# A woven delta rule whose four compute engines follow one written order, with weights split in halves at fixed steps and residual tiles lent out as buffers

## The chip, the cores and the metric

The kernel runs on one core of a Trainium2 chip. The metric is the device time of one execution in microseconds. Five queues matter here: TensorE (PE; its weight loads are listed as PEld), VectorE (DVE), ScalarE (ACT), GpSimd (POOL), and SyncE (SP), which issues the transfers. Each takes its own instructions in the order in which they stand; they meet only through semaphores.

## The reference, cut to what matters

Three transformer blocks of width 1024 on 512 tokens, in float32. The change lies inside the second block, in the gated delta rule and in the products around it:

```
h = layer_norm(x, ln_in_g, ln_in_b)
pool_in, qkv, z, beta_raw, a_raw, gate_a, gate_b = split(h @ w_in)
y_a = multiscale_pool(pool_in) * pool_scale
qkv = silu(causal_depthwise_conv(qkv));  q, k = l2norm(q), l2norm(k)       # 8 heads of 128
u, w = triangular_solve(I + strict(k_beta k^T * decay), [v beta, k_beta e^gc])
for chunk in chunks:                                                       # the recurrence
    v_new = u - w S;  o = qg S + attn v_new;  S = S e^gl + kg^T v_new
y_b = rms_norm(o) * o_norm_w * silu(z)
mixed = sigmoid(gate_a) * y_a + sigmoid(gate_b) * y_b
h = layer_norm(alpha * h + mixed @ w_out, ln1_g, ln1_b)
```

## The kernel before, in words

Activations stand with the 1024 features in eight tiles of 128 partitions and the 512 tokens along the free axis; `X` holds the residual, `hx` the normalized input as pairs of a rounded part and its remainder. A product with a 1024 x 128 block of weights is a **job** of `K.gemm`: for each of eight feature tiles (k-steps) three matmuls of 512 columns (L172 to L174: rounded weights by both parts of the input, remainder of the weights by the rounded part), 24 in all. Its 512-KB block of weights comes through SP into `wst` (two buffers) and is split in two halves of 512 columns: ACT rounds a half into `wh` (L156), POOL takes the remainder into `wl` (L157). There are four buffers of each, that is two jobs' worth.

`block2` runs the delta rule as a weave. `Weave` is a planner that executes while the program is written: generators (`scores`, `tokens`, `blocks`, `inverse`, `recur`, one chain each over the eight heads, and `conv_silu`, `l2`, `out_norm`, `gate` for single tiles) yield the time at which their next step may stand, computed with costs such as `W.on("V", 0.85)`; `W.pe` moves the planner's clock. Steps that are due go first, by rank, and between them the jobs of `JOBS` go k-step by k-step as filler. `JOBS` names 46 jobs: `k`, `q`, `v` of each head, `z` and `g` (the two gates of a head's output), `a2` to `a7` (gate of the pooled part). A job may have a `need`: `k` and `q` of head h wait for the recurrence of head h-4, `v` for `tokens` of head h-1, `z` and `g` for the normalized output.

Before, `tc.manual_schedule` holds only PE and DVE to that order. ACT, POOL and SP are put in order by the scheduling layer, which has its own idea of when things are ready, and `K.wunit` asks for weights early with a raised priority.

Steps that the prediction uses, by line of the profile:

- `conv_silu`: ACT copies the job's PSUM into `cz` (L1379) and scales it into `QK` or `vT` (L1381), after which the PSUM bank is free; three DVE multiply-adds (L1384); Tanh (L1387). `cz` is a new tile each time, whose first three columns POOL clears (L1378).
- `l2`: Square and a rounding on ACT (L1404, L1407), remainder on POOL (`sl`, L1409), two matmuls of column sums (L1411, L1412); for the second of a head's pair a Ln over both (L1419) and two Exp (L1421), each kind behind a table load.
- `inverse`: transposes and products in PSUM `piv` (L1544 to L1573), with copies on ACT (`Xi` L1546, `Yi` L1569) and masks or subtractions on DVE.
- `recur`: per chunk of 128 tokens L1593, DVE, L1599, ACT `vn` (L1603), L1607, DVE `S`, L1616 and L1618 into `po`; its small products go to the one PSUM bank `prc`.
- `out_norm`: copy and Square on ACT (L1629, L1631), the sum over features into `prc` (L1634), Ln and Exp (L1636, L1637) behind a table load each, a multiply on DVE.
- `gate`: Tanh from PSUM into the one buffer `mt` (L1647); for `z` a DVE multiply that reads the PSUM (L1655), then POOL.

PSUM holds two banks `g` for the jobs, two `piv`, two for the sums `m`, one `prc`, one `po`.

Of the kernel before, what the change touches and what calls it, by code (L numbers as in the profile page):

```python
# [9 lines left out]
F32 = mybir.dt.float32  # L10
# [26 lines left out]
JOBS = "k0 q0 v0 k1 q1 a2 a3 v1 k2 q2 a4 v2 k3 q3 a5 v3 z0 k4 q4 g0 v4 z1 k5 q5 g1 v5 z2 k6 q6 g2 v6 k7 q7 z3 v7 g3 z4 g4 z5 g5 a6 z6 g6 a7 z7 g7"  # L37
# [1184 lines left out]
def block2(K, X, entry, es):  # L1222
# [11 lines left out]
    hx = []  # L1234
    for k in range(NT + 1):
        if k == EV[0]:
            for u, o in zip(units, head):
                entry.norm.evict(u, o[:u[0].shape[0]])
        if k < NT:
            affine(K, entry.norm, "ln_in_g", "ln_in_b", hx, k)  # L1240

# [128 lines left out]
    nc.vector.tensor_scalar(ow, K.v("o_norm_w"), 0.25, None, op0=MUL)  # L1370
    W = Weave()
    sums = []
    QK, vT, ci, oTs, mixed = {}, {}, {}, {}, {}

    def conv_silu(ps, ti, y):
        yield W.now + 0.25
        z = pH.tile([P, 3 + T], F32, tag="cz", name=K.nm("cz"))
        nc.gpsimd.memset(z[:, :3], 0.0)  # L1378
# [4 lines left out]
        for k in range(3):  # L1383
            nc.vector.scalar_tensor_tensor(y, v4(z[:, k:k + T]), w(k), y, op0=MUL, op1=ADD)  # L1384
            yield W.on("V", 0.85)
# [6 lines left out]
    def l2(h, y, bias):  # L1392

        if not sums:
            ps = K.pp.tile([P, 2, T], F32, tag="m", bufs=1, name=K.nm("pm"))
        else:
            ps = sums[0][0]
        n = len(sums)
        sums.append((ps, y, bias))
        both = list(sums)  # L1400
        if n:
            sums.clear()
# [7 lines left out]
        yield W.on("P", 1.35)  # L1410
        nc.tensor.matmul(ps[:, n], lhsT=ones_r, rhs=sh, start=True, stop=False)  # L1411
        nc.tensor.matmul(ps[:, n], lhsT=ones_r, rhs=sl, start=False, stop=True)  # L1412
        t = W.pe(0.46)
        W.mark(("sum", h, n), t)
        if not n:
            return
        yield ("sum", h, 0)
        yield t
        nc.scalar.activation(ps, ps, AF.Ln, scale=0.25, bias=K.eps[1e-6])  # L1419
        for k, (ps, y, bias) in enumerate(both):  # L1420
            nc.scalar.activation(ps[:, k], ps[:, k], AF.Exp, scale=-0.5, bias=bias)  # L1421
        yield W.on("A", 5.0)
        for k, (ps, y, bias) in enumerate(both):
            nc.vector.tensor_tensor(y, y, v4(ps[:, k]), MUL)
        W.mark(("QK", h), W.on("V", 1.4))

    def head_in(h, o, ps):

        if o == "v":
            vT[h] = ht("vT", VTB)  # L1430
# [3 lines left out]
        if h not in QK:  # L1434
            QK[h] = pH.tile([P, 4, 2, P], F32, tag="QK", bufs=4, name=K.nm("QK"))
# [8 lines left out]
    def scores(h):  # L1444
# [14 lines left out]
        qk = QK[h]  # L1459
        MT = MTs[h] = ht("MT")  # L1460
# [25 lines left out]
    def tokens(h):  # L1486

        if h > 1:
            yield ("r", h - 2)
        qg = ht("qg")  # L1490
        nc.sync.dma_start(qg, rd[1, h].partition_broadcast(P))
        yield ("QK", h)
        KG = ht("KG")
        VB = ht("VB")
# [21 lines left out]
    def blocks(h):  # L1516
# [6 lines left out]
        for a in range(SB - 1):  # L1523
# [3 lines left out]
            w = W.on("V", 0.42)  # L1527
# [4 lines left out]
    def inverse(h):  # L1532
# [7 lines left out]
        yield W.on("V", 1.2)  # L1540
# [39 lines left out]
    def recur(h):  # L1580
# [6 lines left out]
        O = K.ps("o")  # L1587
        S = None
        for c in range(4):
# [25 lines left out]
            if c:  # L1615
                nc.tensor.matmul(O[:, cc[c]], lhsT=S, rhs=qg[:, cc[c]], start=True, stop=False)  # L1616
                W.pe(0.23)
            nc.tensor.matmul(O[:, cc[c]], lhsT=vn, rhs=AT[:, cc[c]], start=c == 0, stop=True)  # L1618
# [6 lines left out]
    def out_norm(h, O):  # L1625
# [4 lines left out]
        s = K.tmp()  # L1630
        nc.scalar.activation(s, oT, AF.Square)  # L1631
        yield W.on("A", 1.3) + 0.4
        ps = K.ps("rc")
        nc.tensor.matmul(ps, lhsT=K.ones, rhs=s, start=True, stop=True)  # L1634
        yield W.pe(0.86)
        nc.scalar.activation(s, ps, AF.Ln, scale=1.0 / 128, bias=K.eps[1e-6])  # L1636
        nc.scalar.activation(s, s, AF.Exp, scale=-0.5)  # L1637
        yield W.on("A", 3.9)
# [4 lines left out]
    def gate(h, o, ps):  # L1643

        yield W.now + 0.25
        t = ht("mt", MTB)
# [27 lines left out]
    def products(jobs):  # L1674
# [3 lines left out]
        def fetch(j):  # L1678
            for e, us in (("A", 1.3), ("P", 2.8)):
                W.on(e, us)  # L1680
            return K.wunit(I[wname[j[0]]][int(j[1])])
        w = fetch(jobs[0])
        for n, (o, h) in enumerate(jobs):
            h = int(h)
            need = ("o", h) if o in "zg" else ("r", h - 4) if o in "kq" and h > 3 else ("A", h - 1) if o == "v" and h else 0.0
# [4 lines left out]
            nxt = fetch(jobs[n + 1]) if n + 1 < len(jobs) else None  # L1690
            ps = K.gps()
            for k in range(NT):
                K.gemm(ps, hx[k:k + 1], w, off=k * P, first=k == 0, last=k == NT - 1)
                W.pe(0.68)
                if k < NT - 1:
# [3 lines left out]
            w = nxt  # L1699

    with tc.manual_schedule(engines={mybir.EngineType.PE, nc.vector.engine}):
# [6 lines left out]
    mixed = [mixed[h] for h in range(NT)]  # L1708
    K.psum(g=5, m=3)
# [542 lines left out]
```

## Time and profile before

| | us |
|---|---|
| median of 3 runs (2886.43 to 2895.01) | 2893.02 |
| the profiled execution | 2890.26 |
| its span | 2888.5 |
| the weave: first matmul of `k0` to the first of `w_out` | 1111.2 to 1560.6 = 449.4 |

The profiled execution's span is 1.8 us below its own time. The page shows PE at 92% of the whole span and at 6 to 9 tenths in the slices of the weave; in the long products before and after it, PE is at 9 in every slice. PE's busy time is modelled and matmuls overlap, so what is read below is the time in which PE stands idle, what released it, and the granted clock.

### The profile page before, as it was taken

How to read it: one execution, taken by the hardware profiler on the slowest of the kernel's cores; microseconds unless marked ns; L12 is line 12 of the kernel's file. 1: busy time of each engine (PE TensorE's matmuls, PEld its weight loads, DVE VectorE, ACT ScalarE, POOL GpSimd, SP SyncE). 2: the span in 40 equal slices, each digit the busy share in tenths (PEclk: the TensorE clock that was granted, in tenths of full speed). 3: DMA queues.
4: the chain of work that ended last, by engine and by line, in shares of the span. 5: the costliest groups of instructions: out<-in, count | busy, mean ns of one | idle time of the engine just before them, and what ended most of it. 6: DMA issues, size and time to landing. Idle time of an engine off the chain costs nothing.

```text
span 2888.5 us, 34202 instructions
## 1 busy us (share of the span) xinstructions
PE 2667.2 (92%) x12206; PEld 2132.6 (74%) x12206; DVE 1734.2 (60%) x2731; ACT 1308.1 (45%) x2375; POOL 1364.5 (47%) x1071
## 2 busy tenths in 40 slices
PE   7899999599999988889789999999888889999997
PEld 5677777478888866767677788877666678788885
DVE  7889889975342495865853811125877765422246
ACT  4357776433222355556444533332556642322234
POOL 6554432454444454535535544454544344444442
PEclk9999999799999999999999999999999899999999
DMA  3321111132322222222222222232322122222222
GB/s 115 114 86 48 55 44 37 60 116 91 98 96 95 90 73 88 89 74 74 81 60 75 80 95 95 95 110 80 108 83 73 44 81 88 95 95 95 95 95 102
DMA packets 79193, 243.32 MB, mean 84 GB/s; under 512 B 11312, under 2 KB 15320, under 8 KB 79024
## 3 DMA queue, kind: packets, MB, share of 16 engines
q1 hardware_dynamic: 79024, 241.15, 25.6%
q8 instruction: 96, 1.57, 0.2%
q14 instruction: 73, 0.60, 0.1%
HBM read 230.96 MB, written 4.52 MB: 82 GB/s over the span
## 4 chain that ended last, share of the span: by engine, by line
PE 39%; DVE 10%; ACT 2%; issue 1%; POOL 1%; DMA 0%; DVEq 0%; SPq 0%; ACTq 0%; POOLq 0%
PE pg L173 12%; PE pg L172 12%; PE pg L174 12%; DVE p L2061 1%; DVE Z L1526 1%; DVE Zt L1525 0%; DVE X L396 0%; DVE A L2009 0%; PE piv L1551 0%; DVE p L2058 0%; DVE z L2064 0%; POOL wl L157 0%; DVE QK L1384 0%; DVE X L1795 0%; ACT wh L156 0%
## 5 line engine op out<-in xcount | busy, mean ns | idle before, releaser
L157 POOL TENSOR_TENSOR wl<-wst,wh 128x512 fp32r<-128x512 f32 (+1 forms) x808 | 1094.8, 1360 | 1309.6 <-ACT wh L156 1219.6
L156 ACT ACTIVATE wh<-wst 128x512 fp32r<-128x512 f32 (+1 forms) x808 | 501.8, 627 | 1075.1 <-PE pg L173 930.7
L172 PE MATMUL pg<-op,wh 128*128 128x512 f32 (+1 forms) x2008 | 815.9, 407 | 53.5 <-ACT wh L156 20.9
L173 PE MATMUL pg<-op,wh 128*128 128x512 f32 (+1 forms) x2008 | 801.7, 400 | 1.8 <-DVE op L192 1.6
L174 PE MATMUL pg<-op,wl 128*128 128x512 f32 (+1 forms) x2008 | 798.1, 398 | 3.8 <-POOL wl L157 3.8
L172 PEld LDWEIGHTS pg<-op,wh 128*128 128x128 f32 (+1 forms) x2008 | 385.6, 192 | 135.1 <-ACT wh L156 21.5
L174 PEld LDWEIGHTS pg<-op,wl 128*128 128x128 f32 (+1 forms) x2008 | 384.8, 192 | 85.7 <-POOL wl L157 6.1
L173 PEld LDWEIGHTS pg<-op,wh 128*128 128x128 f32 (+1 forms) x2008 | 386.2, 192 | 80.4 <-DVE op L192 4.5
L172 PE MATMUL pg<-hid,wh 128*128 128x512 f32 x688 | 273.1, 397 | 1.3 <-DVE hid L191 1.3
L173 PE MATMUL pg<-hid,wh 128*128 128x512 f32 x688 | 273.0, 397 | 1.2 <-DVE hid L192 1.2
L174 PE MATMUL pg<-hid,wl 128*128 128x512 f32 x688 | 273.2, 397 | 0.0
L733 DVE SCALAR_TENSOR_TENSOR py<-z,vec,py 128x512 f32<-128x512 f32 x240 | 180.2, 751 | 10.9 <-ACT py L731 6.2
L1180 DVE TENSOR_TENSOR X<-X,pg 128x512 f32<-128x512 f32 x56 | 38.5, 688 | 226.9 <-PE pg L174 226.9
L172 PEld LDWEIGHTS pg<-hid,wh 128*128 128x128 f32 x688 | 129.9, 189 | 33.4 <-DVE hid L191 1.8
L173 PEld LDWEIGHTS pg<-hid,wh 128*128 128x128 f32 x688 | 129.9, 189 | 33.2 <-DVE hid L192 1.5
L174 PEld LDWEIGHTS pg<-hid,wl 128*128 128x128 f32 x688 | 129.9, 189 | 31.6 <-issue 0.2
L191 DVE CAST hid<-t 128x512 fp32r<-128x512 f32 x86 | 52.8, 614 | 146.3 <-ACT t L1157 145.6
L1171 DVE SCALAR_TENSOR_TENSOR t<-pg,R 128x512 f32<-128x512 f32 x32 | 22.1, 692 | 84.0 <-PE pg L174 83.9
L998 ACT ACTIVATE P<-ps,s 128x128 f32<-128x128 f32 (+3 forms) x128 | 66.3, 523 | 11.7 <-DVE s L997 9.7
L192 DVE TENSOR_TENSOR hid<-t,hid 128x512 fp32r<-128x512 f32 x86 | 64.6, 751 | 3.0
L997 DVE TENSOR_REDUCE s<-ps 128x1 f32<-128x128 f32 (+3 forms) x128 | 60.2, 483 | 8.2 <-PE ps L996 6.8
L1384 DVE SCALAR_TENSOR_TENSOR QK<-cz,vec,QK 128x512 f32<-128x512 f32 x48 | 50.0, 1053 | 17.5 <-DMA qg<-rowsd 11.3
(521 smaller groups left out, 4395.3 us busy)
## 6 DMA issues: line engine op xcount, KB each, us to landing
wst<-in_w_f_dram SPq DMA_DIRECT2D x64, 512.0 KB
wst<-in_w_up_dram SPq DMA_DIRECT2D x32, 512.0 KB
wst<-in_w_down_dram SPq DMA_DIRECT2D x32, 512.0 KB
wst<-in_w_ga_dram SPq DMA_DIRECT2D x24, 512.0 KB
wst<-in_w_fg_dram SPq DMA_DIRECT2D x22, 512.0 KB
wst<-in_w_fu_dram SPq DMA_DIRECT2D x22, 512.0 KB
wst<-in_w_q_dram SPq DMA_DIRECT2D x16, 512.0 KB
wst<-in_w_out_dram SPq DMA_DIRECT2D x16, 512.0 KB
```

Of the source, the lines that this page charges most:

```text
L156: nc.scalar.activation(h, st, AF.Copy)
L157: nc.gpsimd.tensor_tensor(l, st, h, SUB)
L172: self.nc.tensor.matmul(ps, lhsT=wh, rhs=h[:, sl], start=first and k == 0, stop=False)
L173: self.nc.tensor.matmul(ps, lhsT=wh, rhs=l[:, sl], start=False, stop=False)
L174: self.nc.tensor.matmul(ps, lhsT=wl, rhs=h[:, sl], start=False, stop=last and k == n - 1)
L191: nc.vector.tensor_copy(h, src)
L192: nc.vector.tensor_tensor(l, src, h, SUB)
L733: nc.vector.scalar_tensor_tensor(y, z[:, k:k + T], w(k), y, op0=MUL, op1=ADD)
L997: nc.vector.tensor_reduce(mx[:, h:h + 1], S[:, :L], AX, MAX, negate=True)
L998: nc.scalar.activation(Pt[h][:, :L], S[:, :L], AF.Exp, bias=mx[:, h:h + 1], accum_out=den[:, h:h + 1])
L1180: nc.vector.tensor_tensor(X[:, m], X[:, m], ps, ADD)
L1384: nc.vector.scalar_tensor_tensor(y, v4(z[:, k:k + T]), w(k), y, op0=MUL, op1=ADD)
```

## The change: what it does, and the diff

- ACT and POOL join PE and DVE in `manual_schedule`: all four keep the order in which the weave writes them. SP stays with the scheduling layer.
- A job's weights are no longer fetched by `K.wunit`. `load(n + 2)` issues the transfer at the start of job n; `split(n + 1, 0)` stands after k-step 0 of job n and `split(n + 1, 1)` after k-step 3.
- The layer-normed residual `X` is stored to DRAM (`xkept`) right after it is made and read back after the weave. Between, its eight tiles serve as two more `QK` buffers (six instead of four), a third `KG`, `VB` and `qg`, and a second `vT`. So `k` and `q` need the recurrence of head h-6 and `v` needs `tokens` of h-2.
- `cz` becomes two lasting tiles, cleared once: 2 clearings on POOL instead of 24.
- `out_norm` writes its sum to the bank of `po` and has its own tile `os`; `recur` takes `po` later, once the head before is through (`("n", h - 1)`). `gate` uses the ring of six `t` instead of `mt`.
- `l2` takes turns (`("turn", i)`), and `JOBS` runs `k4` to `v5` ahead of `z0`; the planner's DVE costs go from 0.85 to 1.0 (conv), 0.42 to 0.64 (a pair of `blocks`), 1.2 to 1.7 (`Yi`).

The instructions themselves are the same in number on PE (11963), DVE and ACT; POOL has 22 clearings less, SP 16 transfers of 256 KB more. From the norm behind the weave on, all queues stand as before.

```diff
-JOBS = "k0 q0 v0 k1 q1 a2 a3 v1 k2 q2 a4 v2 k3 q3 a5 v3 z0 k4 q4 g0 v4 z1 k5 q5 g1 v5 z2 k6 q6 g2 v6 k7 q7 z3 v7 g3 z4 ...
+JOBS = "k0 q0 a2 v0 k1 q1 a3 v1 k2 q2 a4 v2 k3 q3 a5 v3 k4 q4 v4 k5 q5 v5 z0 g0 k6 q6 z1 v6 g1 k7 q7 z2 v7 g2 z3 g3 z4 ...
...
             affine(K, entry.norm, "ln_in_g", "ln_in_b", hx, k)
+            nc.sync.dma_start(xkept[k], X[:, k])
...
+    xq = lambda k: X[:, k:k + 2].rearrange("p a t -> p (a t)").rearrange("p (c e t) -> p c e t", c=4, e=2)
+    QKs = [pH.tile([P, 4, 2, P], F32, bufs=1, name=f"QK{i}") for i in range(4)] + [xq(0), xq(2)]
+    three = lambda tag, k: [ht(f"{tag}{i}", 1) for i in range(2)] + [X[:, k]]
+    KGs, VBs, qgs = three("KG", 4), three("VB", 5), three("qg", 6)
+    vTs = [X[:, 7], ht("vT", 1)]
...
-        z = pH.tile([P, 3 + T], F32, tag="cz", name=K.nm("cz"))
-        nc.gpsimd.memset(z[:, :3], 0.0)
+        z = czs[0]
+        czs.reverse()
...
-            w = W.on("V", 0.42)
+            w = W.on("V", 0.64)
...
-        ps = K.ps("rc")
+        ps = K.ps("o")
         nc.tensor.matmul(ps, lhsT=K.ones, rhs=s, start=True, stop=True)
...
-        t = ht("mt", MTB)
+        t = K.tmp()
...
+        def split(n, k):
+            if n < len(jobs):
+                ws.setdefault(n, []).append(K.wsplit(st[n][:, k * WP:(k + 1) * WP]))
+                W.on("P", 1.35, W.on("A", 0.65))
...
-            need = ("o", h) if o in "zg" else ("r", h - 4) if o in "kq" and h > 3 else ("A", h - 1) if o == "v" and h else 0.0
+            need = ("o", h) if o in "zg" else ("r", h - 6) if o in "kq" and h > 5 else ("A", h - 2) if o == "v" and h > 1 else 0.0
...
-            nxt = fetch(jobs[n + 1]) if n + 1 < len(jobs) else None
+            load(n + 2)
+            w = ws.pop(n)
             ps = K.gps()
             for k in range(NT):
                 K.gemm(ps, hx[k:k + 1], w, off=k * P, first=k == 0, last=k == NT - 1)
                 W.pe(0.68)
+                if k in (0, 3):
+                    split(n + 1, k // 3)
...
-    with tc.manual_schedule(engines={mybir.EngineType.PE, nc.vector.engine}):
+    with tc.manual_schedule(engines={mybir.EngineType.PE, nc.vector.engine, nc.scalar.engine, nc.gpsimd.engine}):
...
+    for k in range(NT):
+        nc.sync.dma_start(X[:, k], xkept[k])
```

The orders of two places follow; line numbers of the changed kernel run 13 to 22 higher for the same step (L1381 is L1394, L1419 is L1433, L1599 is L1616, L1634 is L1655). The first is ACT around the first Ln and Exp of `l2` (on `pm`), before; `pg` is the PSUM of a job, `wh` a rounded half of weights:

```order
L1387 ACTIVATE t_2135_10027<-QK_2116_9942 128x512
L156 ACTIVATE wh_2131_10002<-wst_2128_9996 128x512
L1379 ACTIVATE cz_2134_10013<-pg_2122_9953 128x512
L1419 ACT_TABLE_LOAD
L1419 ACTIVATE pm_2103_9887<-pm_2103_9887,eps_1_79 128x1024
L156 ACTIVATE wh_2137_10043<-wst_2136_10041 128x512
L1421 ACT_TABLE_LOAD
L1421 ACTIVATE pm_2103_9887<-pm_2103_9887,lnk_9485 128x512
L1381 ACTIVATE QK_2116_9942<-pg_2122_9953,vec_87 128x4x128
L1421 ACTIVATE pm_2103_9887<-pm_2103_9887,lnq_9483 128x512
```

The same place in the changed kernel:

```order
L1394 ACTIVATE X_91<-pg_2111_9914,vec_87 128x512
L156 ACTIVATE wh_2126_9985<-wst_2110_9912 128x512
L156 ACTIVATE wh_2130_10011<-wst_2122_9963 128x512
L1433 ACT_TABLE_LOAD
L1433 ACTIVATE pm_2118_9955<-pm_2118_9955,eps_1_79 128x1024
L1435 ACT_TABLE_LOAD
L1435 ACTIVATE pm_2118_9955<-pm_2118_9955,lnk_9496 128x512
L1435 ACTIVATE pm_2118_9955<-pm_2118_9955,lnq_9494 128x512
L1392 ACTIVATE cz1_9752<-pg_2123_9965 128x512
L1394 ACTIVATE QK1_9755<-pg_2123_9965,vec_87 128x4x128
L1400 ACTIVATE t_2132_10027<-X_91 128x512
L156 ACTIVATE wh_2133_10032<-wst_2122_9963 128x512
```

Before, the two copies out of one PSUM bank (`cz`, `QK`) stood on both sides of the Ln and the first Exp, with a half of weights between; now the block stands whole, and both copies and the next half of weights stand behind it.

The second place is PE at the end of a stretch with no job to fill it, ahead of the first `v` job after it, before (`piv`, `prc`, `po`, `pm` are the PSUM banks named above):

```order
L1616 MATMUL po_2265_10642<-qg_2086_9771,S_2314_10814 128x128
L1618 MATMUL po_2265_10642<-AT_2144_10073,vn_2323_10840 128x128
L1411 MATMUL pm_2302_10781<-sh_2317_10826,onesr_9735 128x512
L1412 MATMUL pm_2302_10781<-sl_2318_10827,onesr_9735 128x512
L1497 MATMUL piv_2334_10872<-ident_73,QK_2180_10234 128x128 x4
L1573 MATMUL piv_2337_10890<-Yi_2326_10851,T1_2328_10860 128x128 x4
L1634 MATMUL prc_2339_10898<-t_2330_10866,ones_77 128x512
L1508 MATMUL piv_2340_10906<-ident_73,vT_2231_10478 128x128 x4
L1599 MATMUL prc_2342_10915<-VB_2201_10320,Yf_2338_10896 128x128
```

And the longest such stretch of the changed kernel, which stands between `g3` and `z4`; this is its second half:

```order
L1577 MATMUL piv_2714_12627<-T1_2711_12614,Yi_2707_12601 128x128 x4
L1515 MATMUL piv_2717_12638<-ident_73,QK1_9755 128x128 x4
L1585 MATMUL piv_2721_12650<-ident_73,Xi_2718_12644 128x128 x4
L1569 MATMUL piv_2723_12657<-Xi_2718_12644,MT_2569_12040 128x128 x4
L1655 MATMUL po_2724_12662<-os_2716_12634,ones_77 128x512
L1526 MATMUL piv_2728_12675<-ident_73,vT_2079_9764 128x128 x4
L1591 MATMUL piv_2729_12684<-Yi_2722_12655,T1_2725_12664 128x128 x4
L1616 MATMUL prc_2731_12697<-X_91,Yf_2730_12689 128x128
L1483 MATMUL piv_2735_12704<-QK1_9755 128x256 x2
L1624 MATMUL prc_2736_12707<-vn_2732_12699,X_91 128x128
```

The sum of `out_norm` (L1634, now L1655) has left `prc` for `po`, so the next head's first `prc` product (L1599, now L1616) no longer shares a bank with it. Before there are two such unfilled stretches, of 29 and 23 rows of chain products; now there are shorter ones, ahead of `v5`, `z3`, `z4`, `z5` and in `a6`, and the one ahead of `z4` is the longest with 20 rows.

## Rows read from the trace of the kernel before

**Rows 1.** The page: span and instructions.

```profile
span 2888.5 us, 34202 instructions
```

**Rows 2.** Stretches: us, busy time per engine, PEclk, DMA share, GB/s.

```profile
1111.20:1560.60 449.40, 396.79 (x2034) 328.62 (x2033) 277.94 (x573) 237.91 (x402) 219.44 (x184) 0.96 0.25 77
...
1227.00:1262.00 35.00, 25.05 (x134) 20.69 (x133) 23.42 (x61) 19.95 (x33) 11.38 (x11) 0.90 0.18 54
...
1331.00:1381.00 50.00, 38.41 (x175) 30.51 (x175) 34.64 (x68) 29.28 (x51) 28.29 (x25) 0.91 0.29 90
...
1437.00:1466.00 29.00, 18.58 (x95) 15.56 (x94) 14.44 (x38) 16.82 (x27) 9.21 (x7) 0.82 0.23 65
...
1503.00:1560.60 57.60, 57.44 (x309) 48.43 (x310) 17.26 (x32) 27.92 (x47) 31.16 (x24) 1.00 0.23 75
```

**Rows 3.** Waits of PE in the weave: total us, times, longest.

```profile
PE pg L172 <- DVE mt L1655: 7.3, 1, 7.3
PE pg L172 <- ACT QK L1381: 6.8, 2, 3.6
PE pm L1412 <- POOL sl L1409: 5.6, 5, 2.6
PE piv L1551 <- ACT Yi L1569: 5.5, 2, 4.8
PE prc L1599 <- ACT t L1636: 3.8, 2, 3.1
PE piv L1465 <- DVE AT L1470: 3.1, 1, 3.1
PE prc L1607 <- ACT vn L1603: 2.8, 3, 1.7
...
PE piv L1544 <- DVE Yi L1538: 2.4, 2, 2.2
PE prc L1634 <- ACT t L1631: 2.3, 2, 1.8
PE piv L1465 <- DVE Zt L1525: 1.8, 1, 1.8
```

**Rows 4.** Timeline of ACT around the first Ln and Exp: start, us.

```profile
1142.68 0.58 ACT L1379 ACTIVATE cz<-pg 128x512 f32<-128x512 f32 x1
1143.28 1.28 ACT L1419 ACT_TABLE_LOAD   x1
1144.57 1.09 ACT L1419 ACTIVATE pm<-pm,eps 128x1024 f32<-128x1024 f32 x1
...
1146.22 1.28 ACT L1421 ACT_TABLE_LOAD   x1
1147.52 0.66 ACT L1421 ACTIVATE pm<-pm,lnk 128x512 f32<-128x512 f32 x1
1148.10 0.68 ACT L1381 ACTIVATE QK<-pg,vec 128x512 f32<-128x512 f32 x1
```

**Rows 5.** Groups by line, 1000 to 1700 us: busy us, mean ns, idle before.

```profile
L157 POOL TENSOR_TENSOR wl<-wst,wh 128x512 fp32r<-128x512 f32 x163 | 226.0, 1391 | 241.9 <-ACT wh L156 223.8 <-PE pg L173 7.9 <-PE pg L174 3.5
...
L156 ACT ACTIVATE wh<-wst 128x512 fp32r<-128x512 f32 (+1 forms) x162 | 101.0, 626 | 172.5 <-PE pg L173 137.3 <-issue 25.5 <-POOL wl L157 6.0
...
L1525 DVE TENSOR_TENSOR Zt<-B,Z 128x60 f32<-128x60 f32 (+14 forms) x120 | 39.3, 327 | 10.8 <-issue 5.8 <-DMA B<-diag 1.9
L1526 DVE TENSOR_TENSOR Z<-Z,Zt 128x60 f32<-128x60 f32 (+14 forms) x120 | 37.6, 314 | 4.1
```

**Rows 6.** Waits of ACT and of POOL in the weave, columns as in 3.

```profile
ACT t L1387 <- DVE QK L1384: 19.4, 12, 4.7
...
POOL cz L1378 <- DVE vT L1384: 13.4, 6, 3.6
```

**Rows 7.** Timeline of PE within a job at full clock: start, us.

```profile
1257.28 0.39 PE L174 MATMUL pg<-op,wl 128*128 128x512 f32 x1
1257.51 0.40 PE L172 MATMUL pg<-op,wh 128*128 128x512 f32 x1
```

## What I expect

> **What bounds the kernel now.** I read the page first (a span of 2888.5 us [rows 1]), then the weave alone, since nothing outside it changes but transfers. In the weave PE is busy 396.79 of 449.40 us [rows 2], so it stands idle for 52.6 us. DVE is busy 277.94 us, ACT 237.91, POOL 219.44 [rows 2]: no other engine is near its limit over the whole stretch, and the bound is PE plus the holes in it. The view by stretches says where they are: 9.95 us idle in 1227 to 1262, 11.6 in 1331 to 1381, 10.4 in 1437 to 1466 [rows 2], and almost none in the last 57.6 us, where only jobs are left. The mean granted clock is 0.96 over the weave and 0.90, 0.91 and 0.82 in those three stretches [rows 2]. As it is either 1.2 or 2.4 GHz, 0.04 x 449.4 / 0.5 = 36 us run at the lower level, and 26 of them lie in these stretches, that is behind the holes.
>
> Who ended the holes is the view of waits [rows 3]: in every row PE stands at the head of its own queue for one result of ACT, POOL or DVE. Its weights are never in that list. That is the reserve which the change spends: ACT stood idle for 172.5 us ahead of its roundings of weights, most of it until PE gave a buffer back [rows 5], so weights were always split as early as their buffers allowed.
>
> **The change part by part.** A gain is a wait of rows 3 that loses its cause.
>
> Bank of a job behind Ln and Exp: 6.8 us [rows 3]. Before, the scaling copy that frees the bank came 5.4 us after its twin, with the table loads between [rows 4]. Now the block stands whole: 1.28 + 1.09 + 1.28 + 2 x 0.66 = 4.97 us, and behind it both copies, 0.58 + 0.68, so 6.2 us [rows 4]. The other bank covers one job: matmuls start 0.23 us apart at full clock [rows 7], 24 of them are 5.5 us. Some 0.7 us stays each time, 1.4 for two. I take a gain of 5; bounds 0 and 6.8.
>
> Gate of `z`: 7.3 us in one wait [rows 3], for a DVE multiply whose Tanh ACT had put behind such blocks. Now Tanh and multiply stand where the planner puts them and `mt` is no longer one buffer. I take 5, since DVE's queue may still be late; bounds 0 and 7.3.
>
> `prc`: 3.8 us [rows 3], the next head's first product waiting for the Ln that reads the bank. The sum now goes to `po`, so this cause is gone: 3.8. The new wait is that of the recurrence's first product into `po`: for a table load (1.28, [rows 4]) and the Ln, with the five rows of chain products of the order above between the sum and it even in the longest unfilled stretch.
>
> POOL's `sl`: 5.6 us [rows 3]. The clearings of `cz` made POOL wait for DVE (13.4 us in the row shown, [rows 6]) with `sl` and weights queued behind; they are gone. `sl` still has to pass halves of weights of 1.39 us [rows 5]. I take half, 2.8; bounds 0 and 5.6.
>
> ACT's copies on the chain: `Yi` 5.5, `vn` 2.8, Square of `out_norm` 2.3 [rows 3], together 10.6. In the written order PE's filler is placed with the same ACT queue in view, but a copy can still meet a block of 5 us. I take half, 5.3; bounds 0 and 10.6.
>
> DVE: `AT` 3.1, `Yi` 2.4, `Zt` 1.8 [rows 3], together 7.3. A pair of `blocks` takes 0.327 + 0.314 = 0.64 us [rows 5] where the planner reckoned 0.42: over 120 pairs 26 us, 3.3 a head, by which DVE fell behind the plan. The new cost is the measured one. I take 5; bounds 0 and 7.3.
>
> These are 26.9 us of 41.4; the other 11.2 of the 52.6 I leave. The two unfilled stretches become five shorter ones, the longest of 20 rows of chain products against 29 and 23; by idle time per row, 20.35 / 52 = 0.4 us [rows 2], 20 rows are 8 us, and I count no gain on this beyond the terms above.
>
> Clock: in the three stretches PE is busy about 0.72 of the time [rows 2], so 36 us at half speed cost 36 x 0.72 / 2 = 13 us. With the waits halved I take half of it back, 6; bounds 0 and 13.
>
> What it adds. First, **weights come later**. The first half of the next job is split after k-step 0, so it has 7 k-steps, 7 x 3 x 0.23 = 4.8 us, plus what chain products stand between: (396.8 - 46 x 5.5) / 46 = 3.1 us a job on average [rows 2, 7]. Behind a whole block it needs 4.97 + 0.63 + 1.39 = 7.0 us [rows 4, 5]. On average that is covered; in a job without chain products it is 2.2 us short, and PE waits with the whole queue behind it. There are 16 blocks (8 of `l2`, 8 of `out_norm`). The bounds are 0 and 16 x 2.2 = 35 us; before, this cost nothing. I take half a microsecond a block, 8 us, nearer to the lower end because the average job is covered.
>
> What a table load costs decides this. In the trace the load begins 0.02 us after the end of the copy before it, takes 1.28, and the Ln starts 0.01 us behind it [rows 4]. The Trainium skill, page "ScalarE: Activation LUTs", section "What ACT_TABLE_LOAD costs", gives about 1283 ns for the load and another 1380 ns of drain for every switch. The trace agrees with the load and shows no drain. By the page a block would be 4.97 + 2 x 1.38 = 7.7 us, and at 1.4 us more short for each of 16 blocks the forecast would be an estimated 22 us later; I go by the row.
>
> Second, the **residual's way through DRAM**: 8 stores and 8 loads of 256 KB, 4 MB over a weave in which the transfer engines are busy 0.25 of the time at 77 GB/s [rows 2]. A store waits on SP for ACT's scaling of `X`, which the products need anyway, and behind it stand weights for products that need that tile too; this I cost at nothing, and up to 2 us if that cover is gone. A reload waits for the last product that reads the lent tile. Behind the fourth on SP stands the diagonal of head 7, from which its `blocks`, inverse and recurrence follow. I take 1; bounds 0 and 8. The reloads themselves are done long before the first use of `X`, a whole job behind the weave.
>
> Fewer clearings, more buffers and looser needs are in the terms above. Shortened needs alone give nothing, as PE then waits elsewhere.
>
> Sum: -26.9 - 6 + 8 + 1 = -24 us. Against the profiled execution's 2890.26 that is 2866; the median of the runs is 2.8 above it, within their own spread of 2886 to 2895, so I predict **2866**.
>
> **The rivals.**
>
> *The plan holds (0.20).* All 41.4 us and all 13 us of the clock come back and the blocks stay covered: -54, so **2836**. For it: the costs are now those of the trace, and no engine is full. Against it: DVE has 278 us of work of which little falls into the last 57.6 us (17.26 [rows 2]), so before that it is 261 us in some 310, and small lags are hard to avoid.
>
> *The stall only changes its name (0.14).* Weights behind blocks cost 2 us each, 32 in all, and PE's list of waits gets a new first row, `wl`: -26.9 - 6 + 32 + 1 = 0, **2890**. For it: cover and need (4.8 and 7.0 us) are that close.
>
> *Lags travel, slower (0.11).* ACT waited 19.4 us for DVE's convolution in 12 waits, 1.6 us each and up to 4.7 [rows 6], and that harmed no product, as weights were ahead. In one written order a Tanh that waits for DVE holds back the half of weights behind it, then POOL, then the next job on PE, and the delayed job delays the next convolution. With 24 jobs of this kind it decides at (26.9 + 6) / 24 = 1.4 us a job; at 2.5 us it costs 60 - 33 = 27 us, **2917**.
>
> That the change doesn't do what it says is possible in one respect: SP keeps the scheduling layer's order, and a transfer put behind a reload would now hold up strictly ordered engines. Its price is the bound of 8 us above and lies in the forecast's own range.
>
> **How the numbers follow.** The forecast has 0.55: 2852 to 2882 by its unknown terms. 8 in 10 need most of the first rival and most of the second: **2838 to 2891**. A measurement of this kernel tells 0.3%, 8.7 us, from no change. Faster by more than that: the forecast, the first rival and a little of the second, 0.55 + 0.20 + 0.02 = 0.77. Within: 0.12. Slower: 0.11.
>
> **What would show it.** Right: the weave shortens from 449 to about 425 us; PE's waits no longer list `QK`, `mt` and a `prc` bank held by an Ln; idle time sits in the stretches ahead of `z4` and `z5`; the granted clock of the weave rises to 0.97 or more. Wrong: `wl` or `wh` leads PE's waits (second and third rival); ACT's waits for the convolution grow beyond 19.4 us (third); the first `Zt` of head 7 waits for its transfer by more than 3 us (the reload); the stretches outside the weave change by more than 3 us, which no term here foresees.

## The result and the profile after

The changed kernel takes **2861.66 us** (median of 4 runs, 2855.71 to 2863.77); the kernel before, measured beside it, 2892.22 (2886.43 to 2895.01). The ratio is 0.9895, with a 95% interval of 0.9881 to 0.9910: 30.6 us faster. Beside the halves and quarters of the experiments, one of 19 runs of the kernel before took 2925.55 us at a granted clock of 0.897 (the others 2884 to 2899 at 0.964 or more); it counts in the ratios of that group, not in its median of 2889. The profiled execution took 2863.77 us and its span is 2862.0, 26.5 us under that of [rows 1].

First the stretches of the kernel after, to be laid beside [rows 2]: the weave, a hole of the chain, the two holes ahead of `z4` and `z5`, and the end. Columns: us, then busy time of PE, PEld, DVE, ACT and POOL, the granted clock, DMA share, GB/s.

```profile
span 2862.0 us, 34137 instructions
...
1109.63:1535.16 425.53, 390.59 (x2034) 323.70 (x2033) 301.68 (x575) 235.21 (x403) 217.62 (x162) 0.98 0.29 85
1180.00:1225.00 45.00, 37.70 (x186) 30.71 (x186) 41.57 (x67) 24.45 (x43) 26.77 (x20) 0.96 0.31 95
...
1425.00:1470.00 45.00, 34.75 (x198) 28.43 (x199) 30.79 (x79) 20.18 (x35) 17.70 (x14) 0.96 0.35 90
1504.00:1535.16 31.16, 31.16 (x154) 25.88 (x152) 6.11 (x13) 14.54 (x27) 16.73 (x14) 1.00 0.24 75
```

The weave shortened from 449.4 to 425.5 us, which is nearly all of the gain; it starts 1.6 us earlier, and the last 1 us is gained behind it. PE is busy 6.2 us less for the same products (the clock: 0.98 against 0.96) and idle 35 us in place of 52.6. But **DVE is busy for 24 us more** than before, 301.68 against 277.94, for the same operations. In the stretch of 1180 to 1225 it is the fullest engine, 41.57 of 45 us.

Next what PE waits for in the weave of the kernel after; total us, times, longest. It answers to [rows 3].

```profile
PE piv L1569 <- DVE KG L1520: 3.9, 2, 2.4
PE piv L1483 <- DVE AT L1488: 3.8, 1, 3.8
PE piv L1562 <- DVE Yi L1556: 3.5, 4, 0.9
PE piv L1585 <- DVE Xi L1580: 3.3, 4, 1.6
PE prc L1610 <- DVE S L1630: 2.9, 1, 2.9
PE piv L1591 <- DVE Zt L1543: 2.8, 1, 2.8
PE prc L1616 <- DVE Yf L1594: 2.6, 4, 1.4
PE piv L1526 <- DVE X L1520: 2.0, 1, 2.0
PE piv L1591 <- ACT Yi L1587: 2.0, 1, 2.0
PE prc L1624 <- ACT vn L1620: 1.8, 2, 1.4
PE pg L172 <- ACT t L1669: 1.3, 1, 1.3
...
```

Four of the first five rows of [rows 3] are gone: the DVE multiply on `mt`, the bank behind an Ln, POOL's `sl`, the bank of `prc`. The fifth, ACT's `Yi` (now L1587), went from 5.5 to 2.0 us, and a new row, the Tanh of `gate` (ACT `t` L1669), has 1.3 us. No weight, `wh` or `wl`, is in the list. Added up by the engine that was late, PE's waits went from ACT 24.8, POOL 6.2 and DVE 21.9 us to ACT 6.0, POOL 0 and DVE 28.4. The gain came from ACT and POOL, and DVE gave some of it back.

The block of table loads does what the change wrote. A timeline of ACT in the kernel after (start, us), to be laid beside [rows 4]:

```profile
1139.19 1.28 ACT L1435 ACT_TABLE_LOAD   x1
1140.48 0.66 ACT L1435 ACTIVATE pm<-pm,lnk 128x512 f32<-128x512 f32 x1
1141.18 0.66 ACT L1435 ACTIVATE pm<-pm,lnq 128x512 f32<-128x512 f32 x1
1141.76 0.59 ACT L1392 ACTIVATE cz<-pg 128x512 f32<-128x512 f32 x1
1142.24 0.69 ACT L1394 ACTIVATE QK<-pg,vec 128x512 f32<-128x512 f32 x1
```

The two copies that free a job's bank stand together behind the block, 0.48 us apart where it was 5.4 us, and no product waits for them. Of the 24 such pairs this was the only one that a table load split before; the others were 0.48 to 1.05 us apart.

**Where DVE's 24 us come from** is seen when its timeline and POOL's are read together. Of the kernel after, DVE and POOL ahead of the 3.80 us hole that the second row of waits names:

```profile
1183.34 1.73 POOL L1417 TENSOR_TENSOR sl<-t,sh 128x512 fp32r<-128x512 f32 x1
1183.85 1.27 DVE L1543 TENSOR_TENSOR Zt<-B,Z 128x24 f32<-128x24 f32 x1
1185.02 1.31 POOL L157 TENSOR_TENSOR wl<-wst,wh 128x512 fp32r<-128x512 f32 x1
1185.14 1.22 DVE L1544 TENSOR_TENSOR Z<-Z,Zt 128x24 f32<-128x24 f32 x1
1186.28 1.29 POOL L1517 TENSOR_TENSOR qg<-QK,qg 128x512 f32<-128x512 f32 x1
1186.40 1.21 DVE L1543 TENSOR_TENSOR Zt<-B,Z 128x20 f32<-128x20 f32 x1
1187.54 2.48 POOL L157 TENSOR_TENSOR wl<-wst,wh 128x512 fp32r<-128x512 f32 x2
1187.65 1.19 DVE L1544 TENSOR_TENSOR Z<-Z,Zt 128x20 f32<-128x20 f32 x1
1188.87 1.18 DVE L1543 TENSOR_TENSOR Zt<-B,Z 128x16 f32<-128x16 f32 x1
1190.09 0.17 DVE L1544 TENSOR_TENSOR Z<-Z,Zt 128x16 f32<-128x16 f32 x1
1190.18 0.68 DVE L1672 SCALAR_TENSOR_TENSOR ya<-t,ya 128x512 f32<-128x512 f32 x1
...
1191.12 0.41 DVE L1488 TENSOR_TENSOR AT<-piv,D 128x256 f32<-128x256 f32 x1
1191.68 0.89 PE L1483 MATMUL piv<-QK 128*128 128x256 f32 x3 [3.80 <-DVE AT L1488]
```

An operation on 16 numbers per partition takes 1.18 us while POOL works and 0.17 us as soon as POOL has stopped. The slow ones end 0.03 to 0.05 us after a POOL operation does (1183.34 + 1.73 and 1183.85 + 1.27, say): DVE gets one operation in, then POOL the next. Five of them cost 5 us, `AT` comes that much later, and PE stands. So the engines do not meet "only through semaphores", as the section on the chip has it: here a DVE operation is held by a POOL operation whose result it does not need. Of the 240 operations of `blocks`, 195 take 0.19 us on average and 45 take 1.11 us. Operations that have one input in PSUM don't show this: `T<-piv,lev` takes 687 ns in both kernels. The Trainium skill, page "SBUF — State Buffer", section "SBUF: two separate sides", says that VectorE and GpSimd share a port pair under an exclusive lock: a DVE operation with two SBUF inputs and a GpSimd operation that reads SBUF keep each other out for a whole instruction. The trace agrees, with 0.17 and 1.18 us for the same operation.

### The profile page after: what moved, and what is told of

It reads as the page before. It is cut to its first block, busy times and chain, and to the rows that moved or that the text cites. A ratio compares the mean times of both kernels' runs of the same rounds, so it can differ in the third digit from the quotient of the medians.

```text
span 2862.0 us, 34137 instructions
## 1 busy us (share of the span) xinstructions
PE 2656.5 (93%) x12206; PEld 2126.7 (74%) x12206; DVE 1764.7 (62%) x2731; ACT 1305.6 (46%) x2375; POOL 1370.3 (48%) x1049
## 3 DMA queue, kind: packets, MB, share of 16 engines
q1 hardware_dynamic: 81328, 245.35, 26.5%
## 4 chain that ended last, share of the span: by engine, by line
PE 67%; DVE 22%; ACT 5%; issue 3%; DMA 1%; POOL 1%; SPq 0%; DVEq 0%; ACTq 0%; POOLq 0%
PE pg L173 19%; PE pg L172 19%; PE pg L174 19%; DVE p L2097 1%; DVE py L733 1%; DVE Zt L1543 1%; DVE X L396 1%; DVE Z L1544 1%; PE ppt L1016 1%; DMA B<-diag 1%; PE ps L994 1%; DVE ln L337 1%; POOL wl L157 1%; PE po L1022 1%; ACT wh L156 1%
## 5 line engine op out<-in xcount | busy, mean ns | idle before, releaser
L1020 DVE TENSOR_TENSOR PTl<-ppt,PTh 128x512 fp32r<-128x512 f32 x80 | 53.4, 685 | 4.7 <-ACT PTh L1019 4.1
```

The lines of the kernel that those rows point to most:

```text
L1020: nc.vector.tensor_tensor(tl, pt, th, SUB)
```

## The experiments

Three theories were set out first. **A**: the written order of ACT and POOL made the gain. **B**: the planner's numbers did (costs, row of jobs). **C**: DVE's operations grew because POOL works beside them, and this is what limits the kernel now. All times are medians; the ratio is to the kernel before as it was measured beside that group, at 2889 to 2892 us. The kernel after was not run again in the later groups, where the kernel before was 1 to 3 us faster than beside it; so a difference of some 3 us from 2862 means nothing here. The weave is counted from the first product of a job to the first of the mix behind it, and PE's waits in it are summed by the engine that was late.

| kernel | us | ratio to before | weave | PE waits for DVE / ACT / POOL | DVE busy |
|---|---|---|---|---|---|
| before | 2892 | | 449.4 | 21.9 / 24.8 / 6.2 | 277.9 |
| after | 2862 | 0.9881 to 0.9910 | 425.5 | 28.4 / 6.0 / 0 | 301.7 |
| two engines only | 2876 | 0.9934 to 0.9964 | 435.2 | 22.9 / 19.7 / 1.1 | 297.3 |
| old costs | 2866 | 0.9901 to 0.9931 | 429.9 | 31.4 / 6.4 / 1.3 | 295.1 |
| old row of jobs | 2876 | 0.9922 to 0.9977 | 438.7 | 32.9 / 10.4 / 0.8 | 303.7 |
| no remainder on POOL | 2836 | 0.9792 to 0.9828 | 398.6 | 12.1 / 5.3 / 0 | 244.6 |
| remainder in halves | 2856 | 0.9806 to 0.9933 | 418.2 | 24.4 / 5.4 / 0.2 | 291.8 |
| remainder in quarters | 2851 | 0.9779 to 0.9930 | 408.7 | 20.6 / 3.0 / 3.1 | 276.8 |
| weights later | 2879 | 0.9924 to 0.9978 | 441.3 | 34.3 / 4.9 / 5.1 | 307.4 |
| before, in quarters | 2883 | 0.9962 to 0.9987 | 446.8 | 15.9 / 23.9 / 7.7 | 262.9 |
| more POOL work in quarters | 2855 | 0.9860 to 0.9897 | 412.1 | 13.6 / 2.9 / 9.6 | 266.9 |
| no way through DRAM | 2861 | 0.9877 to 0.9914 | 424.3 | 25.8 / 5.5 / 0.2 | 298.4 |
| quarters, true POOL cost | 2847 | 0.9841 to 0.9882 | 405.4 | 16.9 / 4.0 / 0.7 | 284.4 |

### Undoing the parts of the change, one at a time

**ACT and POOL in the layer's order again:**

```diff
-    with tc.manual_schedule(engines={mybir.EngineType.PE, nc.vector.engine, nc.scalar.engine, nc.gpsimd.engine}):
+    with tc.manual_schedule(engines={mybir.EngineType.PE, nc.vector.engine}):
```

> The kernel after, but ACT and POOL take back the scheduling layer's order; only PE and DVE keep the weaver's. Theory A (the written order of ACT and POOL removed the waits on ACT and POOL): the waits on a job's bank, on the Square of the norm, on `sl` and on the copies Yi and vn come back, 15 to 25 us in all, the weave goes from 425 back to 440 us or more and the time from 2862 to 2877 or more. Theory B (the new costs, the other row of jobs and the added buffers made the gain, whoever orders ACT and POOL): the time stays within 5 us of 2862.

Measured: 2876.14 us, so 14.5 us of the gain are lost. The waits on ACT are back, 19.7 us; these are their first row and that of the bank:

```profile
PE prc L1624 <- ACT vn L1620: 13.2, 4, 3.8
...
PE pg L172 <- ACT QK L1394: 1.7, 1, 1.7
```

Theory A holds for about half of the gain. Not in the way expected, though: the bank (`QK` L1394) comes back with 1.7 us and `sl` with 1.1, while the recurrence's copy `vn` takes 13.2 us, more than the 2.8 us of [rows 3]. The trace of this run shows why: in all four cases ACT had stood idle for 3.4 to 4.3 us at an earlier operation of its queue that waited for DVE or POOL (once `cz`, once the Tanh of a convolution, twice `D`, L1468), and `vn` stood behind it. What the written order removes is mostly this, an urgent copy queued behind one whose input is late.

**The planner's DVE costs of before** (1.0, 0.64 and 1.7 us back to 0.85, 0.42 and 1.2):

```diff
-            w = W.on("V", 0.64)
+            w = W.on("V", 0.42)
```

> The kernel after, with the planner's three DVE costs of before (0.85, 0.42 and 1.2 in place of 1.0, 0.64 and 1.7). Theory A (order of ACT and POOL): within 4 us of 2862, since DVE's waits grew in any case. Theory B (costs): DVE falls behind the plan as before, AT, Zt and Yi make PE wait 10 us more and the time is 2872 or more.

Measured: 2866.22, 4.6 us later, between the two and little more than these runs can tell. PE's waits for DVE go from 28.4 to 31.4 us. The costs are worth something, but not the 10 us of theory B.

**The row of jobs of before**, first with the new, looser needs:

```diff
-JOBS = "k0 q0 a2 v0 k1 q1 a3 v1 ... k4 q4 v4 k5 q5 v5 z0 g0 k6 q6 z1 v6 g1 k7 q7 z2 v7 g2 z3 ..."
+JOBS = "k0 q0 v0 k1 q1 a2 a3 v1 ... z0 k4 q4 g0 v4 z1 k5 q5 g1 v5 z2 k6 q6 g2 v6 k7 q7 z3 ..."
```

> The kernel after with the row of jobs of before. Theory A: the row of jobs moves holes but not their sum, within 5 us of 2862. Theory B (the row of jobs spreads the filler better): two long stretches without filler are back, at 0.4 us a row of chain products 52 rows give 20 us of idle time against 12 in the five short ones, so 2870 or more.

Measured: 2875.33. In this run a third convolution starts while two are in flight and overwrites the first one's buffer `cz`, of which there are two (the third copy starts at 1200.4 us, the first one's last multiply-add at 1201.3); its values are then other ones, with the same instructions. It was run again with the need of `v` as before, which keeps the convolutions apart (the expectation names the value tile for this; it was `cz`):

```diff
-            need = ... ("A", h - 2) if o == "v" and h > 1 else 0.0
+            need = ... ("A", h - 1) if o == "v" and h else 0.0
```

> The kernel after with the row of jobs of before, and with the need of a `v` job of before, on the value tile of the head before it (with the looser need this row of jobs overwrites a value tile that is still to be read, which the earlier run of this row did). Theory B (the new row of jobs keeps DVE's work early and spreads PE's filler): 2872 to 2878, as that run. Theory A (the row has no part, the run's time came from its looser need): 2862 within 5 us.

Measured: 2876.42, so 14.8 us of the gain are lost: theory B is right about the row of jobs. What is lost is spread over PE's waits for all engines and the clock (0.96 against 0.98 in the weave).

Taken one by one, the order of ACT and POOL (14.5), the row of jobs (14.8) and the costs (4.6) come to 33.9 us, against 30.6 for the whole (39 when each is set against the kernel before of its own group). Neither A nor B alone made the gain. No run undid the lent tiles with their looser needs, the sum's move from `prc` to `po`, the turns of `l2` or the two lasting `cz`, so what these are worth by themselves is not shown.

**The way of the residual through DRAM:** no stores, no reloads.

```diff
-            nc.sync.dma_start(xkept[k], X[:, k])
...
-        nc.sync.dma_start(X[:, k], xkept[k])
```

> The kernel after without the stores of the residual tiles to DRAM and without their reloads; the lent tiles then hold the buffers' last contents, so the residual is left out of what follows. If the way through DRAM is hidden (no row of the kernel after waits for it, and DVE's waits on the diagonal's transfer are 1.2 us): 2862 within 3 us. If it costs by the bound of the prediction, through the diagonals queued behind it: 2854 to 2858.

Measured: 2861.39, within 0.3 us of the kernel after. The way is hidden, to the 3 us that can be told.

**Weights split later:**

```diff
-                if k in (0, 3):
-                    split(n + 1, k // 3)
+                if k in (4, 6):
+                    split(n + 1, (k - 4) // 2)
```

> The kernel after, with the two halves of the next weights split after k-steps 4 and 6 of a job, not 0 and 3: 3 k-steps (2.1 us) stand between a half's rounding and its first product in place of 7 (4.8 us), against 0.63 + 1.36 = 2.0 us of rounding and remainder. If the reserve at 0 and 3 is wide (the kernel after shows no `wh` or `wl` among PE's waits): waits on `wl` behind the 16 blocks of 5 us only, some 3 us each, 2900 to 2920. If POOL's collisions set the pace, moving its work changes which DVE operations it holds, and the time moves by less than 10 us.

Measured: 2878.97, 17 us later, and neither expectation as it stands: the late weights were to cost 38 us or more, and they show as 1.8 us. PE's waits of this kernel that name a weight or POOL:

```profile
PE pm L1427 <- POOL sl L1417: 3.6, 1, 3.6
PE pg L174 <- POOL wl L157: 1.5, 2, 0.9
PE pg L172 <- ACT wh L156: 0.3, 1, 0.3
```

Of the 16 us by which the weave grew, 3.6 are the row of `sl`, 5.9 are DVE (34.3 us of PE's waits in place of 28.4; 307.4 us busy) and 6.1 are PE's own time for the same products, at a granted clock of 0.95 in place of 0.98. So late weights cost little directly, and the second expectation is right about where the time goes, DVE and POOL, but not about its size. The reserve is not wide, though. From the end of POOL's remainder of a half to the first product that reads it, the median over the 92 halves is 11.7 us in the kernel before, 7.2 after and 3.9 here; under 1 us were 1, 2 and 10 halves.

### What POOL does to DVE

**No remainder of the weights on POOL:** the third product of a step takes the rounded half once more, so the remainder is left out of the result.

```diff
-                ws.setdefault(n, []).append(K.wsplit(st[n][:, k * WP:(k + 1) * WP]))
+                h = K.wp.tile([P, WP], F32R, tag="wh", bufs=WB, name=K.nm("wh"))
+                nc.scalar.activation(h, st[n][:, k * WP:(k + 1) * WP], AF.Copy)
+                ws.setdefault(n, []).append((h, h))
```

> The kernel after without POOL's remainder of the weights in the weave's jobs: the third product of a step takes the rounded half again, so PE has as many products as before, ACT still rounds, POOL has 92 subtractions less (128 us of its 218). The remainder of these weights is left out of the computation. Theory C (DVE's operations got longer, 278 to 302 us, because POOL works beside them): DVE's busy time in the weave falls to 270 us or less, the pair of `blocks` from 727 ns to under 640, DVE's waits on PE from 28 to 15 us or less, the time to 2850 or less. Rival D (they are longer for what they read or for their place, POOL has no part): DVE stays at 295 to 302 us, the pair over 700 ns, the time within 5 us of 2862.

Measured: 2836.34, 25 us under the kernel after, and DVE is busy 244.6 us in place of 301.7. Groups of DVE by line, busy us and mean ns, in the weave of the kernel after:

```profile
L1543 DVE TENSOR_TENSOR Zt<-B,Z 128x60 f32<-128x60 f32 (+14 forms) x120 | 45.8, 382 | 4.1 <-DMA B<-diag 1.2
L1544 DVE TENSOR_TENSOR Z<-Z,Zt 128x60 f32<-128x60 f32 (+14 forms) x120 | 41.3, 345 | 4.1
L1397 DVE SCALAR_TENSOR_TENSOR QK<-cz,vec,QK 128x512 f32<-128x512 f32 x36 | 38.8, 1082 | 11.6 <-ACT QK L1394 11.5
L1556 DVE TENSOR_TENSOR Yi<-Z,lev 128x128 f32<-128x128 f32 x32 | 18.9, 652 | 0.0
L1572 DVE TENSOR_TENSOR T<-piv,lev 128x512 f32<-128x512 f32 x24 | 16.5, 687 | 20.9 <-PE piv L1569 20.9
```

and in the kernel without POOL's remainder:

```profile
L1397 DVE SCALAR_TENSOR_TENSOR QK<-cz,vec,QK 128x512 f32<-128x512 f32 x36 | 30.2, 844 | 13.6 <-ACT QK L1394 13.5
L1543 DVE TENSOR_TENSOR Zt<-B,Z 128x60 f32<-128x60 f32 (+14 forms) x120 | 29.6, 247 | 3.0
L1544 DVE TENSOR_TENSOR Z<-Z,Zt 128x60 f32<-128x60 f32 (+14 forms) x120 | 27.2, 227 | 4.1
L1572 DVE TENSOR_TENSOR T<-piv,lev 128x512 f32<-128x512 f32 x24 | 16.5, 688 | 24.9 <-PE piv L1569 24.9
L1556 DVE TENSOR_TENSOR Yi<-Z,lev 128x128 f32<-128x128 f32 x32 | 10.3, 382 | 0.0
```

What reads two tiles from SBUF got shorter (382 to 247, 345 to 227, 652 to 382, 1082 to 844 ns); what reads one input from PSUM stayed at 687 and 688. Theory C holds, rival D falls. PE's waits for DVE fell from 28.4 to 12.1 us. The pair of `blocks` in the kernel before is 641 ns [rows 5] and its `Yi` is this row, so before paid for the same thing, less:

```profile
L1538 DVE TENSOR_TENSOR Yi<-Z,lev 128x128 f32<-128x128 f32 x32 | 11.5, 419 | 0.0
```

Of DVE's 24 us more in the kernel after, `Zt` and `Z` are 10.2 against [rows 5] and `Yi` is 7.4; the multiply-adds of the convolutions and their product with the Tanh, which read two tiles from SBUF too, are some 8.

**Shorter operations on POOL**, nothing left out: the subtraction of a half of weights in pieces of 256 and of 128 columns.

```diff
-                ws.setdefault(n, []).append(K.wsplit(st[n][:, k * WP:(k + 1) * WP]))
+                s_ = st[n][:, k * WP:(k + 1) * WP]
+                h, l = (K.wp.tile([P, WP], F32R, tag=t, bufs=WB, name=K.nm(t)) for t in ("wh", "wl"))
+                nc.scalar.activation(h, s_, AF.Copy)
+                for i in range(0, WP, 128):
+                    nc.gpsimd.tensor_tensor(l[:, i:i + 128], s_[:, i:i + 128], h[:, i:i + 128], SUB)
+                ws.setdefault(n, []).append((h, l))
```

> The kernel after, with POOL's subtraction of each half of weights in the weave written as two of 256 columns (0.68 us each by the rows of that width elsewhere, against 1.36 for 512), nothing left out. Theory C (a DVE operation with two inputs in SBUF waits for the whole POOL operation that is running, and the two engines take turns; alone an operation of `blocks` takes 0.19 us, in 51 of 240 cases some 1.0): the wait per turn is halved, the pair of `blocks` falls from 727 to some 560 ns, DVE's busy time in the weave by 15 us or more, the time to 2852. Rival D' (DVE only loses a share of its speed while POOL is busy, whatever the size of POOL's operations): DVE's rows and the time stay, 2862 within 4 us.

> As the half, with four subtractions of 128 columns (0.46 us each by the rows of that width, so POOL's part grows from 1.36 to 1.83 us a half of weights). Theory C: the wait per turn falls to a third, the pair of `blocks` to some 470 ns, the time to 2848 unless POOL's 43 us of added work make weights late (then `wl` shows up among PE's waits). Rival D': slower than 2862, as POOL is busy for longer.

Measured: 2856.01 and 2850.72 us. The halves' 6 us under the kernel after are less than these runs can tell, though the weave is 7 us shorter; all runs of the quarters (2844.76 to 2854.38) lie under those of the kernel after (from 2855.71), and of their 11 us some 3 can come from the group. The direction is theory C's, the size is not, and the rows say why. POOL's subtractions and two groups of DVE in the quarter run:

```profile
L1713 POOL TENSOR_TENSOR wl<-wst,wh 128x128 fp32r<-128x128 f32 x356 | 180.6, 541 | 88.8 <-ACT wh L1711 87.9 <-POOL wl L1713 0.9
...
L1543 DVE TENSOR_TENSOR Zt<-B,Z 128x60 f32<-128x60 f32 (+14 forms) x120 | 41.1, 343 | 5.3 <-DMA B<-diag 2.3
...
L1556 DVE TENSOR_TENSOR Yi<-Z,lev 128x128 f32<-128x128 f32 x32 | 11.9, 432 | 0.0
```

`Zt` was expected to fall to some 235 ns, half of the pair's 470, and is at 343. Counting the 240 operations of `blocks` by their length: over 0.3 us there are 45 of 1.11 us in the kernel after, 70 of 0.78 with halves and 104 of 0.51 with quarters. Times what each exceeds 0.19 us by, that is 41, 41 and 33 us. As the two engines take turns, a POOL operation of a quarter of the columns (0.54 us in place of 1.36) holds a DVE operation for less, but there are four times as many turns: a long row of small DVE operations loses about POOL's working time either way. What gets shorter is a single held operation, 1.2 us to 0.4, and that helps the operations that stand alone: `Yi` 652 to 432 ns. A stretch of the quarter run, DVE and POOL (x8 are eight in a row):

```profile
1185.78 4.27 POOL L1713 TENSOR_TENSOR wl<-wst,wh 128x128 fp32r<-128x128 f32 x8
...
1188.39 0.42 DVE L1543 TENSOR_TENSOR Zt<-B,Z 128x12 f32<-128x12 f32 x1
1188.85 0.38 DVE L1544 TENSOR_TENSOR Z<-Z,Zt 128x12 f32<-128x12 f32 x1
1189.27 0.38 DVE L1543 TENSOR_TENSOR Zt<-B,Z 128x8 f32<-128x8 f32 x1
```

Rival D', that only POOL's busy time counts, would have made the quarters slower (POOL is busy 58 us more in the weave); it falls.

**The same quarters in the kernel before** (the same edit where that kernel splits its weights):

> The kernel before, with POOL's subtraction of each half of weights in the weave in four of 128 columns, and nothing else of the change. If long POOL operations cost PE through DVE in either kernel (in before 33 of 240 operations of `blocks` take 1.13 us in place of 0.19, and 21.9 us of PE's waits are DVE's): 6 to 12 us come back here too, 2878 to 2884. If that cost shows only once the waits on ACT are gone: 2889 within 4 us.

Measured: 2882.64, 7 us under the kernel before. DVE loses less there too (277.9 to 262.9 us busy) and PE's waits for it fall from 21.9 to 15.9. So this is a cost of both kernels, not of the change; the change made it larger.

**More of POOL's work in quarters**, on top of the weights', as here for `sl`. The edit also takes one product of `Bb`, the two of `oT` and the remainder of the mix; D, the other product of `Bb` and `qg`, eight operations each, stay whole:

```diff
-        nc.gpsimd.tensor_tensor(sl, s, sh, SUB)
+        for i in range(0, T, 128):
+            nc.gpsimd.tensor_tensor(sl[:, i:i + 128], s[:, i:i + 128], sh[:, i:i + 128], SUB)
```

> The kernel after with the weights' subtractions in four as in the quarter run, and the other POOL operations of the weave on 512 columns (`sl`, the two products of `Bb` and D, `oT`, the remainder of the mix) in four as well. If single waits behind a POOL operation of 1.36 us are what is left of DVE's lateness: 3 to 6 us below the quarter run, 2846. If POOL's own time decides now (the quarter run's waits on `sl` are 3.1 us; some 55 operations by 4 x 0.5 less 1.36 are 35 us more of POOL): the waits on `sl` grow to 6 us or more and the time is 2853 or more.

Measured: 2855.18, not under the quarter run. The wait on POOL says why; first the quarter run, then this one:

```profile
PE pm L1427 <- POOL sl L1417: 3.1, 3, 2.0
```

```profile
PE pm L1431 <- POOL sl L1390: 9.6, 6, 3.4
```

PE's waits for DVE went on falling, 20.6 to 13.6 us, and POOL itself became late, as the second expectation has it: the price of a wait was only moved.

**Quarters with a planner that knows them:** 2.1 us a half of weights in place of 1.35, and a mark that keeps two convolutions at most in flight.

```diff
-                W.on("P", 1.35, W.on("A", 0.65))
+                W.on("P", 2.1, W.on("A", 0.65))
...
+        if n > 2:
+            yield ("cz", n - 2)
```

> The quarter run's kernel with the planner told what POOL's four pieces take (2.1 us a half of weights, 4 x 0.54 by that run, where it reckoned 1.35), and with a mark that makes a convolution wait for the reader of its `cz` buffer. If the quarter run's waits on `sl` (3.1 us) and part of DVE's come from a plan that sees POOL too early: those waits go and the time is 2843 to 2848. If a true cost only moves the holes (a later remainder makes products wait in the plan instead): 2851 within 4 us. If the plan fills with POOL as the late engine: 2857 or more, with `sl` or `wl` in PE's waits.

Measured: 2847.41 us (2845.38 to 2852.00), ratio to before 0.9862 (0.9841 to 0.9882). The two edits were not tried apart. The row of `sl` is 0.7 us now, as the first expectation has it:

```profile
PE pm L1431 <- POOL sl L1421: 0.7, 1, 0.7
```

By its median this is the fastest of the kernels that leave nothing out: its slowest run lies under the fastest of the kernel after, 2855.71, and the two intervals of the ratio only touch. Its 3 us to the quarter run are less than these runs can tell apart.

## Why the prediction was right, and which of its steps was not

The forecast of 2866 us is 4 us from the median, by the case that was given as likeliest. That it is so close is in part luck, as errors of 15 and 19 us cancel. Its parts in the profiled executions:

- **Waits on ACT and POOL: right, and a little too small.** Bank 6.8 of 6.8 us gained (forecast 5), gate 6.0 of 7.3, since the Tanh has 1.3 now (5), `prc` 3.8 of 3.8 (3.8), `sl` 5.6 of 5.6 (2.8), copies on the chain 10.6 down to 4.7, so 5.9 (5.3). The sum is 28.1 in place of 21.9. The residue of 0.7 us behind each block, which the forecast kept, doesn't appear. That the written order gained the bank and `sl` is not shown: with the layer's order of ACT and POOL only 1.7 and 1.1 us of them came back, none of the wait behind `mt` and none of the Ln's on `prc`. The rows fit the other parts that the prediction named for them (no clearings, no single `mt`, the sum in `po`), which no run undid; the order's worth shows in `vn`, at which the prediction put half of 2.8 us.
- **Clock: right.** PE is busy 6.2 us less, forecast 6; the weave's clock is 0.98.
- **Weights split later: 0 in place of +8.** No row names `wh` or `wl`. The term took a half of weights as standing behind a whole block and 2.2 us short; the halves did come later, a median of 7.2 us ahead of their first product in place of 11.7, but none was short, and moved 3 to 4 k-steps later they still cost only 1.8 us.
- **DRAM: 0 in place of +1.** DVE's waits on the diagonals are 1.2 us in three times, 0.7 the longest, and without the way the time is the same to 3 us.
- **DVE: the wrong step.** "The new cost is the measured one. I take 5" of 7.3 us. All of PE's waits for DVE other than the one on `mt`, 14.6 us before, became 28.4: +14 in place of -5. The step took 0.64 us a pair as a property of the operation. It is a mean over operations of 0.19 us and some that stand behind POOL, and it went to 0.73 once the change had set POOL's work elsewhere.

So -28.1 + 14 - 6.2 is -20 for the weave by these steps (rows of ACT and POOL that no step named, 4.2 us, are gone as well), against 23.9 in its length, 26.5 in the span and 30.6 in the medians. The forecast's -24 held because what it gave away on ACT, POOL, the weights and DRAM, some 15 us, was nearly the 19 it missed on DVE. The single runs confirm that the order and the row of jobs made the gain, not the sum of small terms: undoing the order of ACT and POOL takes back half of it.

Two figures of the prediction are off without bearing on its sum. Ahead of the last 57.6 us the weave has 449.4 - 57.6 = 392 us for DVE's 261, not "some 310". And its estimate from the Trainium skill goes on with 1.4 us a block where 7.7 less 4.97 is 2.8; nothing hangs on it, as the kernel after shows no drain either (a load ends at 1140.47 us, the Exp behind it starts at 1140.48). Of its signs, one came only in part: of the 35 us that PE is idle, 10 lie in the stretch around `z4` and `z5`, the rest is spread over the weave.

Of the rivals, that the plan holds (2836) failed mostly on DVE, +14 us where it had -7.3, and on the clock, 6.2 of 13; that the kernel without POOL's remainder takes 2836.34 is a coincidence, as it does less work. That the stall only changes its name to `wl`, and that lags travel, didn't come: ACT's waits for the convolution's Tanh fell from 19.4 us [rows 6] to 6.0, although ACT now keeps a written order. All of ACT's waits for DVE in the weave, those of `l2` included, fell from 29.9 to 20.1.

What of the change raised DVE's busy time from 278 us to 302 isn't settled. It is 295 to 304 with the old costs, the old row of jobs or the old order of ACT and POOL, and 307 with the halves later. The place of the halves between the k-steps may be one part, as moving them moved DVE's time by 6 us; but no run put them back as before, nor the lent tiles, nor two parts at once, and the kernel before with four engines in written order was not run.

## What to carry to other kernels

Before a mean duration from a profile becomes a planner's cost, look at its spread: 195 operations of 0.19 and 45 of 1.11 us are not 240 of 0.36, and the second kind belongs to another engine's queue. Where DVE stands ahead of TensorE with operations that read two tiles from SBUF, keep POOL's operations short, or its work out of those stretches, and tell the planner what the pieces cost. Undo the parts of a large change one by one even when the sum came out: here the order, the row of jobs and the costs each carried a share.

## What the runs showed of the hardware

POOL and DVE take turns operation by operation when POOL's operations and DVE's with two inputs in SBUF stand against each other; DVE's with one input in PSUM kept their 687 ns. What a held operation takes is set by POOL's, not by its own size: 24 and 16 numbers per partition took 1.27 and 1.18 us beside POOL, and 16 took 0.17 alone. Cutting POOL's operations from 512 to 128 columns raised its time for a half of weights from 1.36 to 4 x 0.54 = 2.16 us and cut a single held operation to 0.4 us, but lowered the loss of a long row of small operations only from 41 to 33 us.
